# Matmuls of 512 columns issued as two of 256, in two orders, and three orders for the matmuls of an up product

## The chip, the cores and the metric

The kernel runs on one core of one Trainium2 chip. The metric is the time of one execution on the device, in microseconds. Rows of the profile come from one profiled execution; their times count from its first instruction.

## What is computed

One layer of a decoder for 256 tokens of width 2048, all in fp32:

```python
h = rmsnorm(x, g_mix) @ w_in                       # 2048 -> 5728 columns
z, xbc, dt, q, k, v, qi, ki, wi = split(h)
y_ssd = gated_norm(ssd(silu(conv(xbc)), dt), z)    # state space heads
y_att = sparse_attention(q, k, v, qi, ki, wi)      # top 64 keys by an indexer
x = x + concat([y_ssd, y_att]) @ w_out             # 2048 -> 2048
u = rmsnorm(x, g_mlp) @ w_up                       # 2048 -> 8192
return x + square(relu(u)) @ w_down                # 8192 -> 2048
```

Nearly all arithmetic lies in the four products with `w_in`, `w_out`, `w_up` and `w_down`.

## The kernel before

**Exact products in two parts.** TensorE multiplies operands of type fp32r. Each fp32 operand is split into a high part of that type (a cast, on ScalarE) and a low part (the rest, a subtraction on VectorE). For weights `operands` does this, per piece of 128 x 1024 elements that SyncE's DMA queue loads into `raw`: lines 119, 122 and 123 write `raw`, `whi` and `wlo`. There are 4 buffers for `raw` and 5 each for `whi` and `wlo`. A product is then the sum of three terms: high x high, low x high, high x low.

**Two forms of product.** `product` has tokens on partitions: the stationary operand is a slice of 128 tokens of the activations, the moving one is a row of weights, `n` columns wide. For each of 16 steps `kt` over the 2048 terms, and for each half `b` of the tokens, `part` issues three matmuls (lines 141 to 143) into the accumulator `acc[b]`, one PSUM bank of 512 fp32 columns. It serves the input projection (activations `hx`; five blocks of 512 columns, `k`, `q0`, `q1`, `z0`, `z1`, and two of 304, `m0`, `m1`), the output projection (`yah`, `yal` and `ysh`, `ysl`) and the down products (`uh`, `ul`). In the very last block, which has a `tail`, the second half of the tokens is accumulated in two halves of 256 columns in two banks (`acc`, `acc_t`), and the last four steps of each part are done one part after the other, so that each can be added and stored while the next runs.

`product_t` has columns on partitions: the stationary operand is a block of 128 x 128 weights, the moving one the activations, whose high and low parts lie side by side (`x`, 512 columns: 256 high, 256 low). Line 181 multiplies the high weights by all 512 columns, line 182 the low weights by the high 256 columns, into the upper half of the same bank. `total` adds the two halves of the bank later. It serves the blocks `qi` and `xbc` of the input projection (from `hx`) and the up products (from `x2x`, which takes the place of `hx`).

**Order of the work.** TensorE's program is in the order in which the code issues it. Small tasks (norms, transposes, index scores on lines 434 and 435, state space, attention on lines 586 to 611) run beside the large products: `step`, called once per `kt`, moves each of them on. In the MLP no task is left. The MLP goes by quarters `q` of its width: `up(0)`, then `up(q)` and `down(q - 1)` in turn, and `down(3)`. An `up` is eight calls of `product_t` (the first of all is made earlier, as `first`), a `down` four calls of `product`; 32 and 16 in all.

Of the kernel before, what the change touches and what calls it, by code (L numbers as in the profile page):

```python
# [16 lines left out]
P = 128  # L17
D = 2048
T = 256
NB = T // P  # L20
KT = D // P
DFF = 8192
EPS = 1e-6
# [9 lines left out]
# columns of the input projection, in the order of the program's blocks  # L33
# [15 lines left out]
# columns of the per-partition vectors  # L49
# [6 lines left out]
# columns of the vectors that all partitions hold  # L56
# [9 lines left out]
def hymba_kernel(ctx: ExitStack, tc: tile.TileContext, xn, xt, w_in, w_out, w_up, w_down, vcol, vrow, out):  # L66
    nc = tc.nc
# [11 lines left out]
    # ---- what runs beside the large products: each task yields the number of steps to wait, or what has to be done  # L79
    Y = dict(k=20, q=8, cb=11, pv=3, gate0=10, gate1=7, res=3, rr=16, conv=9, sc=2, dec=3, y=3)  # L80
    tasks = []
    done = set()
# [26 lines left out]
    # ---- blocks of a product with 2048 terms; operands in two parts that the tensor engine multiplies exactly  # L109
    def operands(src, n, load=None):  # L110
        """a piece of a block, [128, n], in its two parts"""
# [20 lines left out]
    def product(src, n, left, load=None, tail=None):  # L132
        """tokens on partitions: out[b][:, :n]; with a tail the parts end one after the other: each is handed over as
        (b, columns, out)"""
        acc = accumulators()
        last = KT if tail is None else KT - 4

        def part(kt, out, b, wh, wl):
            s = slice(b * P, (b + 1) * P)
            ah, al = left(kt)  # L140
            nc.tensor.matmul(out, ah[:, s], wh, start=(kt == 0), stop=False)  # L141
            nc.tensor.matmul(out, al[:, s], wh, start=False, stop=False)  # L142
            nc.tensor.matmul(out, ah[:, s], wl, start=False, stop=(kt == KT - 1))  # L143
# [27 lines left out]
    def product_t(src, right):  # L171
        """two blocks of 128 columns on partitions: the two halves' sum is the product"""
        acc = accumulators()
        for i in range(4):
            hi, lo = operands(src[i], 1024)
            c = i % 2
            for k in range(8):
# [3 lines left out]
                nc.tensor.matmul(acc[c], hi[:, s], x, start=(kt == 0), stop=False)  # L181
                nc.tensor.matmul(acc[c][:, T:], lo[:, s], x[:, :T], start=False, stop=(kt == KT - 1))  # L182
# [4 lines left out]
    def total(dst, acc):  # L187
        """dst[:, c, :] = the sum of the two halves"""
# [4 lines left out]
    # ---- the exponential's table, and matrix products until the first operands are there: the engine's clock rises  # L193
# [8 lines left out]
    # ---- loads of the activations, in turn with the first weights  # L202
# [43 lines left out]
    # ---- constants  # L246
# [13 lines left out]
    def rsqrt(dst, src, scale, name, v=nc.vector):  # L260
        """dst = (src * scale + EPS) ** -0.5; the sign of the estimate changes with each step"""
# [13 lines left out]
    # ---- the statistics of the rows  # L275
# [559 lines left out]
```

## Time and profile before

| | |
|---|---|
| median of 3 runs | 1122.08 us (1121.83 to 1122.97) |
| span of the profiled execution | 1121.0 us, first to last instruction |
| TensorE, matmul rows | 1106.8 us, 99% of the span, 5690 matmuls |
| TensorE, weight loads | 935.5 us, 5690 loads |
| VectorE | 705.7 us, 63% |
| ScalarE | 529.8 us, 47% |
| weights loaded | 205.27 MB by DMA, 183 GB/s on average |

The rows come from the profiled execution, whose span is some 1.1 us shorter than the median of the runs. Matmuls overlap, and the end of a matmul's row is modelled; where successive matmuls start is recorded. A line such as L141 is a line of the kernel before. In a row of the timeline, the shape `128*128 128x512` is that of the output's partitions and of the weights, and then of the moving operand: 512 columns.

### The profile page before, as it was taken

What the parts mean: (1) busy time and instruction counts of PE and PEld (TensorE: products, weight loads), DVE (VectorE), ACT (ScalarE), POOL (GpSimd) and SP (SyncE); (2) the same over time, 40 slices, a digit from 0 to 9 for tenths busy, and PEclk for the clock granted to TensorE, in tenths of its full rate; (3) what the DMA queues carried; (4) which work ended last, traced back from release to release, by engine and by line L of the source; (5) the groups of instructions that cost most, each with busy time, mean ns of one, the idle gap of its engine ahead of it and who ended that gap; (6) DMA issues with size and microseconds to landing.
All of it is one profiled execution on the core that took longest, in us unless ns stands there. A gap on an engine that the chain in (4) does not pass through costs nothing.

```text
span 1121.0 us, 14940 instructions
## 1 busy us (share of the span) xinstructions
PE 1106.8 (99%) x5690; PEld 935.5 (83%) x5690; DVE 705.7 (63%) x964; ACT 529.8 (47%) x725; POOL 68.6 (6%) x72
## 2 busy tenths in 40 slices
PE   7999998999999999999999999999999999999998
PEld 5888887788888888888888888888888888888887
DVE  8896889677765566565655446565555565455543
ACT  6555663646665454444443334444334444333331
POOL 7210114122000000000000000000000000000000
PEclk9999999999999999999999999999999999999999
DMA  7665443653465555556566556666666665656662
GB/s 238 210 198 193 156 133 114 225 164 116 147 209 187 187 176 189 188 189 188 189 188 195 189 189 188 188 189 190 195 194 190 188 187 189 189 190 197 212 207 77
DMA packets 61497, 205.27 MB, mean 183 GB/s; under 512 B 7025, under 2 KB 9329, under 8 KB 61425
## 3 DMA queue, kind: packets, MB, share of 16 engines
q1 hardware_dynamic: 61280, 204.26, 57.5%
q8 instruction: 45, 0.74, 0.3%
q14 instruction: 28, 0.22, 0.1%
q10 hardware_dynamic: 144, 0.05, 0.0%
HBM read 202.19 MB, written 2.10 MB: 182 GB/s over the span
## 4 chain that ended last, share of the span: by engine, by line
PE 92%; DVE 4%; DMA 2%; issue 1%; ACT 1%; SPq 0%; POOL 0%; DVEq 0%; ACTq 0%
PE acc L181 26%; PE acc L142 16%; PE acc L143 16%; PE acc L141 16%; PE acc L182 13%; DVE wlo L123 1%; DMA raw<-in_w_in 1%; DVE bc L477 1%; PE ps_y L548 1%; DVE hx L224 1%; DVE sc L441 1%; PE ps_sr L632 0%; PE ps_l L586 0%; PE ps_o L611 0%; PE ps_dec L539 0%
## 5 line engine op out<-in xcount | busy, mean ns | idle before, releaser
L123 DVE TENSOR_TENSOR wlo<-raw,whi 128x1024 fp32r<-128x1024 f32 (+2 forms) x392 | 473.4, 1209 | 381.5 <-ACT whi L122 378.6
L122 ACT CAST whi<-raw 128x1024 fp32r<-128x1024 f32 (+2 forms) x392 | 399.1, 1018 | 516.5 <-PE acc L142 252.6
L181 PE MATMUL acc<-x2x,whi 128*128 128x512 f32 x1024 | 358.8, 393 | 0.0
L182 PE MATMUL acc<-x2x,wlo 128*128 128x256 f32 x1024 | 285.7, 279 | 0.0
L181 PEld LDWEIGHTS acc<-x2x,whi 128*128 128x128 f32 x1024 | 191.9, 187 | 46.0
L142 PE MATMUL acc<-whi,ul 128*128 128x512 f32 (+1 forms) x512 | 199.1, 389 | 0.0
L143 PE MATMUL acc<-wlo,uh 128*128 128x512 f32 (+1 forms) x512 | 199.1, 389 | 0.0
L141 PE MATMUL acc<-whi,uh 128*128 128x512 f32 (+1 forms) x512 | 197.4, 386 | 0.0
L182 PEld LDWEIGHTS acc<-x2x,wlo 128*128 128x128 f32 x1024 | 191.9, 187 | 0.1
L141 PEld LDWEIGHTS acc<-whi,uh 128*128 128x128 f32 x512 | 96.1, 188 | 21.1
L142 PEld LDWEIGHTS acc<-whi,ul 128*128 128x128 f32 x512 | 96.2, 188 | 20.9
L181 PE MATMUL acc<-hx,whi 128*128 128x512 f32 x320 | 113.6, 396 | 0.0
L143 PEld LDWEIGHTS acc<-wlo,uh 128*128 128x128 f32 x512 | 96.2, 188 | 19.1
L142 PE MATMUL acc<-whi,hx 128*128 128x512 f32 (+1 forms) x224 | 84.4, 377 | 5.6 <-DVE hx L224 5.6
L182 PE MATMUL acc<-hx,wlo 128*128 128x256 f32 x320 | 89.4, 279 | 0.0
L143 PE MATMUL acc<-wlo,hx 128*128 128x512 f32 (+1 forms) x224 | 83.3, 372 | 3.1 <-DVE wlo L123 3.1
L141 PE MATMUL acc<-whi,hx 128*128 128x512 f32 (+1 forms) x224 | 85.8, 383 | 0.0
L181 PEld LDWEIGHTS acc<-hx,whi 128*128 128x128 f32 x320 | 60.1, 188 | 13.6
L182 PEld LDWEIGHTS acc<-hx,wlo 128*128 128x128 f32 x320 | 60.0, 188 | 0.0
L142 PEld LDWEIGHTS acc<-whi,hx 128*128 128x128 f32 x224 | 42.2, 188 | 18.8 <-DVE hx L224 12.2
L143 PEld LDWEIGHTS acc<-wlo,hx 128*128 128x128 f32 x224 | 42.2, 188 | 10.7 <-DVE wlo L123 4.2
L141 PEld LDWEIGHTS acc<-whi,hx 128*128 128x128 f32 x224 | 42.2, 188 | 7.7 <-issue 0.7
(224 smaller groups left out, 857.9 us busy)
## 6 DMA issues: line engine op xcount, KB each, us to landing
raw<-in_w_up SPq DMA_DIRECT2D x128, 512.0 KB, 3.6
raw<-in_w_down SPq DMA_DIRECT2D x128, 512.0 KB, 3.6
raw<-in_w_in SPq DMA_DIRECT2D x72, 512.0 KB, 3.5
raw<-in_w_out SPq DMA_DIRECT2D x32, 512.0 KB, 3.5
raw<-in_w_in SPq DMA_DIRECT2D x16, 304.0 KB, 2.9
raw<-in_w_in SPq DMA_DIRECT2D x16, 256.0 KB, 4.0
xT<-in_xt SPq DMA_DIRECT2D x16, 128.0 KB, 3.3
xr<-in_xn SPq DMA_DIRECT2D x4, 512.0 KB, 6.1
```

Source lines behind the costliest of these rows:

```text
L122: nc.scalar.copy(hi[:, s], raw[:, s])
L123: nc.vector.tensor_tensor(lo[:, s], raw[:, s], hi[:, s].bitcast(F32), op=OP.subtract)
L141: nc.tensor.matmul(out, ah[:, s], wh, start=(kt == 0), stop=False)
L142: nc.tensor.matmul(out, al[:, s], wh, start=False, stop=False)
L143: nc.tensor.matmul(out, ah[:, s], wl, start=False, stop=(kt == KT - 1))
L181: nc.tensor.matmul(acc[c], hi[:, s], x, start=(kt == 0), stop=False)
L182: nc.tensor.matmul(acc[c][:, T:], lo[:, s], x[:, :T], start=False, stop=(kt == KT - 1))
L224: nc.vector.scalar_tensor_tensor(hx[:, kt, T:], xT, vcp("g_mix", kt), hx[:, kt, :T].bitcast(F32), op0=OP.mult, op1=OP.subtract)
L441: nc.vector.scalar_tensor_tensor(sc[:, :nk], rl[:, i, :nk], wis[:, b, h:h + 1], neg[:, T - nk:] if first else sc[:, :nk], op0=OP.mult, op1 ...
L477: nc.vector.scalar_tensor_tensor(o[:, j, :], pad[:, j, k:k + T], vcp("conv_w", 12 * k + ct), o[:, j, :], op0=OP.mult, op1=OP.add)
L548: nc.tensor.matmul(pt[:, 64 * i:64 * i + 64], m[i // 4][:, i % 4, :], xdt[:, c, 64 * h:64 * h + 64], start=True, stop=True)
```

## The change

A matmul of 512 columns in `part` is issued as two of 256, each of which names the same stationary operand. Order 0 does the three terms on the first half of the columns and then on the second; order 1 does each term on both halves before the next term. Blocks of 304 columns, and the halves of 256 in the last block, stay single. The input and output projections take order 0; the down products take order 0 in quarters 0 and 2 and order 1 in quarters 1 and 3. In `product_t`, order 0 is the code of before. Order 1 issues the high weights' matmul of 512 columns as two of 256. Order 2 takes two steps `kt` together: two matmuls with high weights, then two with low ones. The up products take order 0 in quarters 0 and 3, order 1 in quarter 1 and order 2 in quarter 2; the blocks `qi` and `xbc` take order 0. Comments and descriptions were removed too.

```diff
-    def product(src, n, left, load=None, tail=None):
+    def product(src, n, left, load=None, tail=None, order=0):
...
             ah, al = left(kt)
-            nc.tensor.matmul(out, ah[:, s], wh, start=(kt == 0), stop=False)
-            nc.tensor.matmul(out, al[:, s], wh, start=False, stop=False)
-            nc.tensor.matmul(out, ah[:, s], wl, start=False, stop=(kt == KT - 1))
+            w = out.shape[1]
+            cs = [slice(0, w // 2), slice(w // 2, w)] if w == 512 else [slice(0, w)]
+            terms = [(ah, wh), (al, wh), (ah, wl)]
+            calls = [(i, c) for c in cs for i in range(3)] if order == 0 else [(i, c) for i in range(3) for c in cs]
+            for at, (i, c) in enumerate(calls):
+                x, y = terms[i]
+                nc.tensor.matmul(out[:, c], x[:, s], y[:, c], start=(kt == 0 and at == 0),
+                                 stop=(kt == KT - 1 and at == len(calls) - 1), skip_group_check=True)
...
-    def product_t(src, right):
+    def product_t(src, right, order=0):
...
-                nc.tensor.matmul(acc[c], hi[:, s], x, start=(kt == 0), stop=False)
-                nc.tensor.matmul(acc[c][:, T:], lo[:, s], x[:, :T], start=False, stop=(kt == KT - 1))
+                end = kt == KT - 1
+                if order == 0:
+                    nc.tensor.matmul(acc[c], hi[:, s], x, start=(kt == 0), stop=False)
+                    nc.tensor.matmul(acc[c][:, T:], lo[:, s], x[:, :T], start=False, stop=end)
+                elif order == 1:
+                    nc.tensor.matmul(acc[c][:, :T], hi[:, s], x[:, :T], start=(kt == 0), stop=False, skip_group_check=True)
+                    nc.tensor.matmul(acc[c][:, T:], hi[:, s], x[:, T:], start=False, stop=False, skip_group_check=True)
+                    nc.tensor.matmul(acc[c][:, T:], lo[:, s], x[:, :T], start=False, stop=end, skip_group_check=True)
+                elif k % 2 == 1:
+                    x0 = right(kt - 1)
+                    s0 = slice((k - 1) * P, k * P)
+                    nc.tensor.matmul(acc[c], hi[:, s0], x0, start=(kt == 1), stop=False)
+                    nc.tensor.matmul(acc[c], hi[:, s], x, start=False, stop=False)
+                    nc.tensor.matmul(acc[c][:, T:], lo[:, s0], x0[:, :T], start=False, stop=False)
+                    nc.tensor.matmul(acc[c][:, T:], lo[:, s], x[:, :T], start=False, stop=end)
...
-            total(r, first if q + j == 0 else product_t(w_up[8 * q + j], x2))
+            total(r, first if q + j == 0 else product_t(w_up[8 * q + j], x2, q % 3))
...
-            acc = product(w_down[4 * q + j], 512, lambda kt: (u[0][:, kt, :], u[1][:, kt, :]), tail=add if end else None)
+            acc = product(w_down[4 * q + j], 512, lambda kt: (u[0][:, kt, :], u[1][:, kt, :]), tail=add if end else None, order=q % 2)
```

## Rows read from the trace of the kernel before

**Rows 1.** Engines of the page: busy us, share of the span, instructions.

```profile
PE 1106.8 (99%) x5690; PEld 935.5 (83%) x5690; DVE 705.7 (63%) x964; ACT 529.8 (47%) x725; POOL 68.6 (6%) x72
```

**Rows 2.** Windows: input projection's last blocks, up products, down products.

```profile
core 0: us, PE busy (x) PEld busy (x) DVE busy (x) ACT busy (x) POOL busy (x), PEclk, DMA share, GB/s
200.00:320.00 120.00, 120.00 (x579) 98.33 (x579) 86.34 (x141) 72.40 (x120) 16.05 (x12) 1.00 0.49 155
410.00:580.00 170.00, 170.00 (x975) 148.23 (x974) 105.94 (x135) 81.18 (x110) 0.00 (x0) 1.00 0.59 187
940.00:1095.00 155.00, 155.00 (x682) 127.29 (x681) 80.12 (x73) 60.21 (x60) 0.00 (x0) 1.00 0.63 199
```

**Rows 3.** Waits: who waited for whom, total us, times, longest us.

```profile
PE acc L142 <- DVE hx L224: 5.6, 15, 1.0
```

**Rows 4.** Timeline of TensorE, a down product: first and last of 54 matmuls.

```profile
599.64 0.39 PE L143 MATMUL acc<-wlo,uh 128*128 128x512 f32 x1
...
611.77 0.39 PE L142 MATMUL acc<-whi,ul 128*128 128x512 f32 x1
```

**Rows 5.** Timeline of TensorE, the last down product: rounds of nine, then halves alone.

```profile
1105.25 0.39 PE L141 MATMUL acc<-whi,uh 128*128 128x512 f32 x1
...
1109.35 0.39 PE L141 MATMUL acc<-whi,uh 128*128 128x512 f32 x1
...
1114.83 0.28 PE L141 MATMUL acc<-whi,uh 128*128 128x256 f32 x1
...
1116.08 0.28 PE L143 MATMUL acc<-wlo,uh 128*128 128x256 f32 x1
...
1117.44 0.28 PE L143 MATMUL acc_t<-wlo,uh 128*128 128x256 f32 x1
```

**Rows 6.** Timeline of TensorE, input projection: 30 of 304 columns, 27 of 512.

```profile
45.91 0.30 PE L143 MATMUL acc<-wlo,hx 128*128 128x304 f32 x1
...
50.00 0.30 PE L142 MATMUL acc<-whi,hx 128*128 128x304 f32 x1
...
206.68 0.39 PE L143 MATMUL acc<-wlo,hx 128*128 128x512 f32 x1
...
212.77 0.40 PE L142 MATMUL acc<-whi,hx 128*128 128x512 f32 x1
```

**Rows 7.** Timeline of TensorE, output projection: first and last of 28 matmuls.

```profile
329.81 0.39 PE L141 MATMUL acc<-whi,ysh 128*128 128x512 f32 x1
...
335.99 0.39 PE L141 MATMUL acc<-whi,ysh 128*128 128x512 f32 x1
```

**Rows 8.** Timeline of TensorE, an up product: the first matmuls and the 37th.

```profile
519.61 0.39 PE L181 MATMUL acc<-x2x,whi 128*128 128x512 f32 x1
519.84 0.28 PE L182 MATMUL acc<-x2x,wlo 128*128 128x256 f32 x1
519.96 0.39 PE L181 MATMUL acc<-x2x,whi 128*128 128x512 f32 x1
...
525.91 0.39 PE L181 MATMUL acc<-x2x,whi 128*128 128x512 f32 x1
```

**Rows 9.** Timeline of TensorE, index scores: first and fifth of five matmuls.

```profile
114.20 0.28 PE L434 MATMUL ps_s<-kih,qis 128*128 128x256 f32 x1
...
114.68 0.28 PE L434 MATMUL ps_s<-kih,qis 128*128 128x256 f32 x1
```

**Rows 10.** Groups by form, one line of three: count, busy us, mean ns, idle.

```profile
L141 PE MATMUL acc<-whi,uh 128*128 128x512 f32 x496 | 193.0, 389 | 0.0
...
L141 PE MATMUL acc<-whi,hx 128*128 128x512 f32 x160 | 66.2, 414 | 0.0
...
L141 PE MATMUL acc<-whi,yah 128*128 128x512 f32 x64 | 25.9, 405 | 0.0
```

**Rows 11.** The instructions of line 435: weight loads and their duration in ns.

```profile
L435 PEld LDWEIGHTS ps_s<-kil,qis x32: 187/189/192, 108.8 to 169.8; 128*128 128x128 f32 x32
```

**Rows 12.** Pieces of the chain, start us, us: plain fp32 matmuls of 256 and 128 columns.

```profile
272.87 1.73 PE ps_o L611 x8
...
298.07 0.87 PE ps_pt L603 x8
```

## The prediction

> **What bounds the kernel now.** I read the table of engines first. TensorE's matmul rows cover 99% of the span [rows 1]. A busy matmul row is a model of overlapping instructions, so the number to read is not its length but the distance from one start to the next. Before that, the stretches: in the input projection's last four blocks, in the up products and in the down products TensorE has no gap at all, its granted clock is 1.00 (the 2.4 GHz level), and VectorE and ScalarE are busy for 39 to 72% of the time [rows 2]. So a nanosecond more or less per matmul goes straight into the end time, in nearly all of the kernel. The one place among the changed products where it does not is the first block ("k"): there TensorE waits 15 times for the low part of the activations, `hx` from VectorE [rows 3], so its 96 matmuls have cover.
>
> Then the starts, in the timeline. Durations in this text are first start to last start over the number of steps between, all in the profiled execution (span 1121.0 us; the three timed runs have a median of 1122.08, so about 1.1 us lies around the span, and I carry that over).
>
> - Down products, 512 columns: 599.64 to 611.77 is 53 steps, 228.9 ns each [rows 4].
> - The end of the kernel already runs 256-column matmuls in a down product, because the last block hands its parts over one by one. 1114.83 to 1117.44 is 23 steps: 113.5 ns. Further ahead, where three matmuls of 512 alternate with six of 256, a round takes (1109.35 - 1105.25)/3 = 1.367 us; less 3 x 228.9 that leaves 113.3 ns for one of 256 [rows 5]. I take 113.4.
> - Input projection, 512 columns: 206.68 to 212.77 is 26 steps, 234.2 ns. The 304-column blocks of the same product: 45.91 to 50.00 is 29 steps, 141.0 ns [rows 6].
> - Output projection: 329.81 to 335.99 is 27 steps, 228.9 ns [rows 7].
> - Up products: a 512 and a 256 together, 519.61 to 525.91, 18 pairs, 350.0 ns [rows 8].
> - The index scores, 256 columns, each weight used twice in a row and the halves of a bank in turn: 114.20 to 114.68 is four steps, 120 ns [rows 9].
>
> So two halves are not simply one whole: in the down products 2 x 113.4 = 226.8 is below 228.9, and the index rate doubled, 240, is far above it. The whole question is which of these rows the new 256-column matmuls resemble.
>
> **Part 1: the split in `part`.** What is split are all matmuls of width 512; 304 and the tail's 256 stay. Counts come from the groups by form, three lines each: down 3 x 496 = 1488, output projection 3 x (64 + 64) = 384 (the group for `ysh` is as large as that for `yah`), input projection 3 x 160 = 480 [rows 10]. Every half loads its weights anew: the score matmuls on line 435 use the weights that line 434 has just used, and have 32 loads of their own for 32 matmuls [rows 11]. So loads double with the matmuls. The tail's rows contain that already: one load for each 256, and at the seam between two halves the same `uh` twice.
>
> *Down, order 0 (quarters 0 and 2, 768) and order 1 (quarters 1 and 3, 720).* Order 0 is what the tail does, three terms on one half and then three on the other, same operands; only the bank is shared now. I take 113.4: 226.8 - 228.9 = -2.1 ns. Order 1 sends each weight twice, in turn to the two halves, which in this kernel only the index scores do, at 120 with other operands. Bounds for it: -2.1 and +11.1 ns. The operands are the tail's and the loads are the same, so it is nearest to the tail: -2.1. Together 1488 x -2.1 = -3.1 us (order 1 at its upper end: +8.0 instead of -1.5 us).
>
> *Output projection.* No 256 there, but its 512 has the down products' pace to 0.1 ns: 384 x -2.1 = -0.8 us; bounds -0.8 and 384 x 11.1 = +4.3.
>
> *Input projection.* Its pace is slower, so the tail's price need not hold. A line through its own 304 (141.0) and 512 (234.2) has 0.448 ns per column and gives 119.5 at 256; the up products' 256, between its neighbours, shows 0.12 us at the rows' two decimals [rows 8]. I take 119: 238 - 234.2 = +3.8 ns. The block "k" (96) has cover: a half less is done before the wait for `hx`, and VectorE sets the pace. If that cover were gone it would add 96 x 3.8 = 0.4 us. The other four blocks, 384: +1.5 us. Bounds: 113.4 gives -2.8, 120 gives +2.2.
>
> **Part 2: the up products.** Quarters 0 and 3 (order 0) are unchanged. Order 1 in quarter 1: 8 products of 32 groups, 256 groups, each 512 + 256 becoming three of 256. Cost of one: the slope between the down products' two widths is (228.9 - 113.4)/256 = 0.451 ns per column; 768 columns of a pair make 346.4, the remaining 3.6 ns are shared by two matmuls, so 256 columns cost 115.5 + 1.8 = 117.3, and three cost 351.9 against 350.0. 256 x 1.9 = +0.5 us. Bounds: three at 113.4 give -2.5, three at 120 give +2.6. Order 2 in quarter 2 only regroups four matmuls, two of 512 and then two of 256; count, columns and loads stay, and `hi` and `lo` are used later, not earlier. I take 0; were each switch of width what costs the 3.6 ns, half of the switches would go: 256 x -1.8 = -0.5 us, and I allow the same upwards.
>
> Nothing else moves. The weights' DMAs, the casts and subtractions and the tasks' places are per piece or per row of `kt`, and those did not change. VectorE and ScalarE get the same work in the same time; a half-matmul frees nothing earlier, as a piece of weights is still free after its last matmul.
>
> **Sum:** -3.1 - 0.8 + 1.5 + 0.5 + 0 = -1.9 us on 1121.0, a span of 1119.1; with what lies around it, about 1120.2. I forecast 1120.
>
> A rule that speaks against even this small gain: the Trainium skill, in "TensorE: Matmul & The Clock Gate", section "Back-to-back issue gap", gives a stream of warm matmuls as columns over 2.4 plus 2.5 ns, so that each split would cost 2.5 ns and the change some 6 us. Here the two halves are 2.1 ns below the whole, and a 512 is at 228.9 where the rule has 215.8; the trace disagrees on both.
>
> **The rivals.**
>
> 1. *The halves run at the tail's pace everywhere.* For: the tail shows the same 113.4 between matmuls of 512 and among halves alone. Against: the 256s of the up products and of the index scores are slower. Input -2.8, up order 1 -2.5, order 2 -0.5, down and output -3.9: -9.7 us, 1112.4. Chance 0.12.
> 2. *Order 1 pays the index rate:* a weight sent twice, or the two halves of a bank in turn, costs 120. For: rows 9. Against: there the step from a repeated weight to a new one is as long as the step between repeats. Down order 1 then +8.0 instead of -1.5: 1129.7, slower. From 114.7 ns for a 256 there the forecast's gain is gone (1440 x 1.3 = 1.9 us), from 116.3 the kernel is slower by over 0.2%. Chance 0.10.
> 3. *A fixed price for each instruction.* Plain fp32 pieces of the chain show a little of one: eight of 256 columns take 1.73 us, 216.3 ns each, eight of 128 take 0.87, 108.8 each [rows 12]: two halves cost 1.3 ns more than a whole. The 304 and 512 of the input projection, drawn down to no columns, leave 141.0 - 304 x 0.448 = 4.8 ns. Were 4.8 the price of every added matmul: (1488 + 384 + 384 + 256) x 4.8 = +12.1 us, 1134. Against: rows 5. Chance 0.05. Set against a cost of nothing per added matmul it decides from 0.9 ns (2512 x 0.9 = 2.2 us).
> 4. *The tail is special* because its halves lie in two banks, and every new 256 costs 119.5: down and output 1872 x 10.1 = +18.9, input +1.8, up +2.2: 1145. Against: 1114.83 to 1116.08, 11 steps that all write one bank, are 113.6 ns apart. Chance 0.05.
>
> **How the numbers follow.** My own case has 0.68. Its terms of the input and up products move it by 3 us either way, so its own range is 1117 to 1123. What a measurement of this kernel can tell from no change is about 0.2%, 2.2 us: faster means below 1119.8. My case lies just beside that line: I give 0.31 of its 0.68 to faster, 0.33 to the same, 0.04 to slower. With the rivals: faster 0.31 + 0.12 = 0.43, same 0.33, slower 0.04 + 0.20 = 0.24. The range for 8 in 10 takes my case, most of rival 1, and the lower prices of rivals 2 and 3 (order 1 partly at the index rate): 1113 to 1127.
>
> **What would show it.** In the timeline after, steps between starts: down, quarters 0 and 2: 113.4; quarters 1 and 3: 113.4 if I am right, about 120 under rival 2; output projection 113.4; input projection near 119; up quarter 1 near 117.3, a group of three at 352; up quarter 2 700 for four, as before. TensorE should stay without gaps in all of these stretches and its loads count as many as its matmuls; a gap at regular distances would be a thing I have not priced. The prediction is wrong if the down products' halves are not below 114.4, where their gain is gone, or if the input projection's halves keep to the tail's pace.

## The result, and the profile after

The changed kernel takes 1135.47 us (median of 4 runs, 1134.7 to 1136.5) against 1122.02 us for the kernel before in the same comparison (1121.83 to 1122.97): a ratio of 1.012, with a 95% interval of 1.0107 to 1.0133. It is slower, and lies outside the range of 1113 to 1127. The profiled executions have spans of 1132.9 and 1121.0 us. A single run lies some 1.8 us above its own span, and the profiled execution before was one of the slower ones, so the medians differ by 13.5 us and the two spans by 11.9. What follows accounts for the 11.9; the first row of its table is where the two differences part.

The table of engines of the kernel after, beside [rows 1]:

```profile
PE 1121.2 (99%) x8298; PEld 1063.8 (94%) x8298; DVE 705.2 (62%) x964; ACT 529.8 (47%) x725; POOL 68.7 (6%) x72
```

TensorE has 2608 instructions more, which is the count of the prediction (1488 + 384 + 480 + 256), and as many weight loads. The other engines do the same work in the same time. The windows of the kernel after follow: the three stretches of [rows 2], then 60 us inside each of the four down quarters.

```profile
core 0: us, PE busy (x) PEld busy (x) DVE busy (x) ACT busy (x) POOL busy (x), PEclk, DMA share, GB/s
200.00:320.00 120.00, 120.00 (x958) 116.08 (x957) 85.09 (x139) 71.93 (x119) 16.40 (x12) 1.00 0.49 154
410.00:580.00 170.00, 170.00 (x1189) 158.67 (x1188) 104.73 (x137) 79.85 (x110) 0.00 (x0) 1.00 0.60 185
940.00:1095.00 155.00, 155.00 (x1294) 153.93 (x1293) 79.20 (x74) 59.36 (x59) 0.00 (x0) 1.00 0.62 194
600.00:660.00 60.00, 60.00 (x512) 60.00 (x511) 29.94 (x28) 22.61 (x22) 0.00 (x0) 1.00 0.61 187
780.00:840.00 60.00, 60.00 (x532) 60.00 (x531) 31.10 (x28) 23.38 (x23) 0.00 (x0) 1.00 0.61 193
960.00:1020.00 60.00, 60.00 (x511) 60.00 (x511) 29.91 (x27) 22.69 (x22) 0.00 (x0) 1.00 0.59 185
1050.00:1110.00 60.00, 60.00 (x512) 60.00 (x511) 30.09 (x27) 22.43 (x22) 0.00 (x0) 1.00 0.67 206
```

In all of these windows TensorE is without a gap and its granted clock is 1.00, as before. The last four rows hold the surprise: the same number of columns per matmul, on the same kind of operands, gives 532 matmuls in 60 us in quarter 1 and 511 or 512 in the others. Quarter 1 is order 1, but so is quarter 3.

The timeline of TensorE gives the steps and where each stretch begins. First the start of the first down product in the kernel before, and of the up product behind it:

```profile
586.81 0.40 PE L141 MATMUL acc<-whi,uh 128*128 128x512 f32 x1
...
674.72 0.40 PE L181 MATMUL acc<-x2x,whi 128*128 128x512 f32 x1
```

Then the kernel after. Rows with x2 are two matmuls of one form that the view shows as one.

```profile
193.89 0.40 PE L147 MATMUL acc<-whi,hx 128*128 128x256 f32 x2
...
208.28 0.40 PE L147 MATMUL acc<-whi,hx 128*128 128x256 f32 x2
...
211.80 0.40 PE L147 MATMUL acc<-whi,hx 128*128 128x256 f32 x2
...
314.19 0.47 PE L147 MATMUL acc<-whi,yah 128*128 128x256 f32 x1
...
329.76 0.28 PE L147 MATMUL acc<-whi,ysh 128*128 128x256 f32 x1
...
334.00 0.28 PE L147 MATMUL acc<-whi,ysh 128*128 128x256 f32 x1
...
408.31 0.40 PE L188 MATMUL acc<-x2x,whi 128*128 128x512 f32 x1
...
539.84 0.28 PE L191 MATMUL acc<-x2x,whi 128*128 128x256 f32 x1
...
542.72 0.28 PE L191 MATMUL acc<-x2x,whi 128*128 128x256 f32 x1
...
590.96 0.28 PE L147 MATMUL acc<-whi,uh 128*128 128x256 f32 x1
...
599.79 0.28 PE L147 MATMUL acc<-whi,uh 128*128 128x256 f32 x1
...
602.97 0.28 PE L147 MATMUL acc<-whi,uh 128*128 128x256 f32 x1
...
681.41 0.40 PE L197 MATMUL acc<-x2x,whi 128*128 128x512 f32 x1
...
720.28 0.39 PE L197 MATMUL acc<-x2x,whi 128*128 128x512 f32 x1
...
722.40 0.39 PE L197 MATMUL acc<-x2x,whi 128*128 128x512 f32 x1
...
771.87 0.39 PE L147 MATMUL acc<-whi,uh 128*128 128x256 f32 x2
...
799.75 0.39 PE L147 MATMUL acc<-whi,uh 128*128 128x256 f32 x2
...
802.92 0.28 PE L147 MATMUL acc<-wlo,uh 128*128 128x256 f32 x1
...
858.91 0.40 PE L188 MATMUL acc<-x2x,whi 128*128 128x512 f32 x1
...
948.52 0.28 PE L147 MATMUL acc<-whi,uh 128*128 128x256 f32 x1
...
1126.60 0.28 PE L147 MATMUL acc<-whi,uh 128*128 128x256 f32 x1
...
1129.19 0.28 PE L147 MATMUL acc_t<-whi,ul 128*128 128x256 f32 x1
```

Steps, worked out as in the prediction (last start less first start, over the steps between):

- Down, quarter 0: 599.79 to 602.97 is 27 steps, 117.8 ns. Quarters 2 and 3 have the same.
- Down, quarter 1: 799.75 to 802.92 is 28 steps, 113.2 ns.
- The tail of the last block, whose matmuls were not touched: 1126.60 to 1129.19 is 22 steps, 117.7 ns. Before it was 113.5 [rows 5].
- Output projection: 329.76 to 334.00, 36 steps, 117.8 ns.
- Input projection: 208.28 to 211.80, 30 steps, 117.3 ns.
- Up product, order 1: 539.84 to 542.72 is eight groups of three halves, 360.0 ns each, where a pair took 350.0 [rows 8].
- Up product, order 2: 720.28 to 722.40 is three groups of four, 706.7 ns each. By the starts in the trace, to the nanosecond, the four steps take 232.5, 231.7, 117.5 and 125.0 ns on the average; in order 0 a 512 takes 232.0 and a 256 takes 118.0. So the extra 6.7 ns lie behind the second low matmul, ahead of the next 512.

I call 113.3 the short step and 117.8 the long step from here on. From the starts of the stretches, before against after:

| Stretch | before, us | after, us | difference | predicted |
|---|---|---|---|---|
| all ahead of the last four input blocks | 195.37 | 193.89 | -1.48 | 0 |
| last four input blocks | 119.60 | 120.30 | +0.70 | +1.5 |
| output projection | 91.75 | 94.12 | +2.37 | -0.8 |
| up quarters 0 and 1 (1: order 1) | 180.09 | 182.65 | +2.56 | +0.5 |
| down quarter 0 | 87.91 | 90.45 | +2.54 | -0.8 |
| up quarter 2 (order 2) | 89.61 | 90.45 | +0.85 | 0 |
| down quarter 1 | 87.90 | 87.04 | -0.86 | -0.8 |
| up quarter 3 | 89.64 | 89.61 | -0.03 | 0 |
| down quarters 2 and 3, to the end | 179.16 | 184.37 | +5.21 | -1.5 |

The sum is +11.9. The first row is scatter, not the change. In it, block `k` takes 31.7 us from its first matmul to the first of the next block, where it took 32.4 before; but after_again, a second execution of the changed kernel (below), has 32.6, and the kernels below that leave `k` whole have 31.8 to 32.5. No effect of the split shows there. TensorE waits for `hx` as before, in the view of the waits, beside [rows 3]:

```profile
PE acc L147 <- DVE hx L242: 5.1, 14, 1.2
```

The rest of the first row is in blocks that the change leaves alone; it took 158.2 us before and 157.2 after, and lies between 157.1 and 158.5 in the profiled executions of all kernels here. Without the first row the table adds up to +13.3 us, close to the 13.5 by which the medians differ.

### The profile page after: what moved, and what is told of

Same layout as the page of the kernel before. It is cut to its first block, busy times and chain, and to the rows that moved or that the text cites. A ratio compares the mean times of both kernels' runs of the same rounds, so it can differ in the third digit from the quotient of the medians.

```text
span 1132.9 us, 20157 instructions
## 1 busy us (share of the span) xinstructions
PE 1121.2 (99%) x8298; PEld 1063.8 (94%) x8298; DVE 705.2 (62%) x964; ACT 529.8 (47%) x725; POOL 68.7 (6%) x72
## 4 chain that ended last, share of the span: by engine, by line
PE 94%; DVE 3%; DMA 1%; issue 1%; ACT 1%; SPq 0%; POOL 0%; DVEq 0%; ACTq 0%
PE acc L147 49%; PE acc L188 16%; PE acc L189 8%; PE acc L192 3%; PE acc L191 3%; PE acc L193 3%; PE acc L198 3%; PE acc L197 3%; PE acc L200 1%; PE acc L199 1%; DMA raw<-in_w_in 1%; DVE wlo L123 1%; DVE bc L495 1%; PE ps_y L566 1%; DVE sc L459 1%
## 5 line engine op out<-in xcount | busy, mean ns | idle before, releaser
L147 PE MATMUL acc<-whi,ul 128*128 128x256 f32 x1008 | 242.0, 279 | 0.0
L147 PE MATMUL acc<-whi,uh 128*128 128x256 f32 x1008 | 241.9, 278 | 0.0
L147 PE MATMUL acc<-wlo,uh 128*128 128x256 f32 x1008 | 241.5, 278 | 0.0
L188 PE MATMUL acc<-x2x,whi 128*128 128x512 f32 x512 | 179.6, 393 | 0.0
L147 PEld LDWEIGHTS acc<-whi,uh 128*128 128x128 f32 x1008 | 172.1, 188 | 0.0
L147 PE MATMUL acc<-whi,hx 128*128 128x256 f32 (+1 forms) x768 | 149.3, 292 | 5.1 <-DVE hx L242 5.1
L188 PEld LDWEIGHTS acc<-x2x,whi 128*128 128x128 f32 x512 | 95.9, 187 | 22.8
L147 PE MATMUL acc<-wlo,hx 128*128 128x256 f32 (+1 forms) x384 | 110.3, 287 | 1.8 <-DVE wlo L123 1.8
L189 PEld LDWEIGHTS acc<-x2x,wlo 128*128 128x128 f32 x512 | 95.9, 187 | 0.0
L192 PE MATMUL acc<-x2x,whi 128*128 128x256 f32 x256 | 72.4, 283 | 0.0
L191 PE MATMUL acc<-x2x,whi 128*128 128x256 f32 x256 | 71.8, 280 | 0.0
```

The source lines that it names most:

```text
L147: nc.tensor.matmul(out[:, c], x[:, s], y[:, c], start=(kt == 0 and at == 0), stop=(kt == KT - 1 and at == len(calls) - 1), skip_group_chec ...
L191: nc.tensor.matmul(acc[c][:, :T], hi[:, s], x[:, :T], start=(kt == 0), stop=False, skip_group_check=True)
L192: nc.tensor.matmul(acc[c][:, T:], hi[:, s], x[:, T:], start=False, stop=False, skip_group_check=True)
```

## The experiments

The down products are more than half of the loss, and the puzzle: one code, two steps. Four theories stood in the expectations. **Entry theory:** what TensorE did just before a stream of halves sets its step, and the stream keeps it. **Order theory:** order 0 or order 1 sets it. **Chance theory:** it falls anew in each execution. **Place theory:** it goes with the buffer that holds `uh` and `ul`, which change places with every quarter. The quarters follow each other as up 0, up 1, down 0, up 2, down 1, up 3, down 2, down 3.

Kernels run in rounds have a ratio with its 95% interval; the others were run once beside their profile, and of these I use the stretches and steps. With whole matmuls down 0 takes 87.9 us; all halves at the short step make that 87.0, at the long step 90.5. The runs come from several chips; lead_a, lead_b and lead_c share one, lead_d and lead_e another, and the steps of down_o0's quarters were the same on two chips (lead512 and slots on the second).

**after_again.** The changed kernel a second time, unchanged.

> The changed kernel once more, for a second trace. Entry theory (the step of a stream of 256-column matmuls is settled by what TensorE did just before the stream and is then kept): every stretch repeats its step, quarter 1's down product 113.3 ns, the three others 117.8. Chance theory (each execution falls into one of the two steps anew): at least one of the four down products is at the other step; its time moves by 3.3 us (768 matmuls of 256 columns x 4.4 ns) for each.

1135.6 us, span 1133.8. Every stretch from the output projection on has its length of the first profile within 0.06 us. The chance theory falls: which quarter is short belongs to the program. The repeated runs further below agree: the four of down_o0 lie within 0.7 us and the nine of lead_d within 1.3, and one quarter at the other step would move a run by 3.4. The other runs with leads were executed once each.

**down_o1 and down_o0.** Only the down products are split, in order 1 throughout or in order 0 throughout. The diff is down_o1; down_o0 has `order=0` in the last line.

```diff
-    def product(src, n, left, load=None, tail=None, order=0):
+    def product(src, n, left, load=None, tail=None, order=None):
...
-            cs = [slice(0, w // 2), slice(w // 2, w)] if w == 512 else [slice(0, w)]
+            cs = [slice(0, w // 2), slice(w // 2, w)] if w == 512 and order is not None else [slice(0, w)]
...
-            total(r, first if q + j == 0 else product_t(w_up[8 * q + j], x2, q % 3))
+            total(r, first if q + j == 0 else product_t(w_up[8 * q + j], x2))
...
-            acc = product(w_down[4 * q + j], 512, lambda kt: (u[0][:, kt, :], u[1][:, kt, :]), tail=add if end else None, order=q % 2)
+            acc = product(w_down[4 * q + j], 512, lambda kt: (u[0][:, kt, :], u[1][:, kt, :]), tail=add if end else None, order=1)
```

> Only the down products are split, all in order 1; projections and up products are those of before. Order theory (order 1 runs at 113.3 ns, order 0 at 117.8): 1488 x (226.6 - 228.9) = -3.4 us, 1118.6, all four quarters at 113.3. Entry theory: each down product is entered from an up product as before, which in the changed kernel led to 117.8 in quarter 2, so 117.8 in all: 1488 x 6.7 = +10.0 us, 1132.

> Only the down products are split, all in order 0. Order theory: 117.8 ns in all quarters, 1488 x 6.7 = +10 us, 1132, and 13 us slower than all in order 1. Entry theory: also 117.8, also 1132, no different from all in order 1. The rule of the prediction (113.4 as in the tail): 1118.6.

down_o1: 1128.89 us (ratio 1.0058, 1.0043 to 1.0073). down_o0: 1128.85 us (1.0058, 1.0041 to 1.0075). In both, down 0 is 2.54 us longer, down 1 is 0.86 shorter and down 2 and 3 are 5.22 longer. The windows of down_o1 in quarters 0 and 1:

```profile
600.00:660.00 60.00, 60.00 (x512) 60.00 (x511) 30.11 (x27) 22.85 (x22) 0.00 (x0) 1.00 0.56 186
780.00:840.00 60.00, 60.00 (x532) 60.00 (x531) 31.12 (x28) 23.45 (x23) 0.00 (x0) 1.00 0.58 194
```

Order 1 has both steps, and order 0 has the same two in the same places: the order theory falls. Quarter 1 is the short one although the up product ahead of it is now the same as ahead of the others, so the simplest form of the entry theory, that the kind of up product decides, falls as well. The 1132 us expected from it was 3 us too long, by that quarter.

**swap.** The changed kernel with the orders of the down products exchanged, `order=(q + 1) % 2`.

> The changed kernel with the two orders exchanged between the quarters of the down products: 0 where 1 was and 1 where 0 was. Order theory: quarters 0 and 2 (now order 1) at 113.3 ns, quarters 1 and 3 at 117.8. Entry theory: nothing moves, quarter 1 stays at 113.3 behind the up product in order 2, the others at 117.8, time within 1 us of the changed kernel.

1135.49 us, span 1133.7. All stretches are those of the changed kernel; quarter 1 is short in order 0 too.

**lead512.** down_o0 with the first step `kt` of each quarter's first block left whole, so that six matmuls of 512 lead in.

```diff
-            cs = [slice(0, w // 2), slice(w // 2, w)] if w == 512 and order is not None else [slice(0, w)]
+            cs = [slice(0, w // 2), slice(w // 2, w)] if w == 512 and order is not None and kt >= whole else [slice(0, w)]
...
-            acc = product(w_down[4 * q + j], 512, lambda kt: (u[0][:, kt, :], u[1][:, kt, :]), tail=add if end else None, order=0)
+            acc = product(w_down[4 * q + j], 512, lambda kt: (u[0][:, kt, :], u[1][:, kt, :]), tail=add if end else None, order=0, whole=1 if j == 0 else 0)
```

> Only the down products split, all in order 0, but for the first of the 64 steps over the terms in each quarter: its six matmuls stay 512 wide. Entry theory (the step is settled where the stream of halves begins): behind matmuls of 512 the halves lock at 113.3 ns, as they did in the last block of the kernel before, in all four quarters: 1464 x (226.6 - 228.9) = -3.4 us, span 1117.6, run 1118.8. Place theory (it hangs on where uh and ul lie): no difference from the run without the lead, quarters 0, 2 and 3 at 117.8, quarter 1 at 113.3, 1128.9.

1128.48 us (1.0055, 1.0039 to 1.0072): a miss. The steps are those of down_o0. A few whole matmuls in front do not clear whatever sets the step.

**half_b1.** down_o0 with only the second token block split, so that halves run between whole matmuls everywhere: the condition for the split becomes `w == 512 and order is not None and b == 1`.

> Only the down products split, and there only the second half of the tokens: in every step three matmuls of 512 and then six of 256, which is what the last block of the kernel before did for most of its length. Entry theory: each run of halves is entered from 512s, so 1.367 us for each step as there, against 6 x 228.9 = 1.373: 244 steps x -6.4 ns = -1.6 us, 1120.5. If halves are at 117.8 whatever stands before them: 244 x 6 x 3.35 ns = +4.9 us, 1127.

1125.18 us (1.0029, 1.0018 to 1.004): a miss again. The halves take 117.8 ns in quarters 0, 2 and 3 and 113.3 in quarter 1, six in a row between whole ones; the stretches differ by +1.28, -0.43 and +2.68 us, half of down_o0's. So the step is not lost when the stream is broken by 512s. The tail of the kernel before is just such a mixture [rows 5]: that it ran at 113.3 is one of two possible outcomes, not its nature.

**slots.** down_o0 with the two buffers of `uh` and `ul` exchanged, by one more allocation ahead of the first quarter.

```diff
+        if q == 0:
+            for nm in ("uh", "ul"):
+                z = mlp.tile([P, KT, T], F32R, name=nm)
+                nc.gpsimd.memset(z[:, 0, :].bitcast(F32), 0.0)
```

> Only the down products split, all in order 0, with the two buffers of uh and ul exchanged between the quarters (a buffer is cleared in part and given back ahead of quarter 0, so that quarters 0 and 2 use the second and 1 and 3 the first). Place theory: the step goes with the buffer, quarters 0 and 2 at 113.3 ns, quarter 1 at 117.8; span about 1125.3. Entry theory: quarter 1 stays the fast one, span as without the exchange, 1127 to 1128.

1129.59 us, span 1127.8; quarter 1 is still the short one. The place theory falls.

**lead_small.** down_o0 with one plain fp32 matmul of 128 columns, whose result is unused, ahead of each down quarter. It is two instructions.

```diff
     def down(q, u):
+        pt = mp("ps_lead")
+        nc.tensor.matmul(pt[:, :P], ident, ident, start=True, stop=True)
```

> Only the down products split, all in order 0, with one small plain fp32 product of 128 columns into a spare bank ahead of each down product (its result isn't used). Entry theory: the shift at the entry changes the step of at least one quarter; which one isn't foreseen; each quarter that changes moves the span by 3.4 us. Place theory: no quarter changes, and the span grows by under 1 us for the eight small matmuls.

1129.59 us, span 1127.8. Quarter 1 has turned long and quarter 3 short. The timeline of lead_small where quarters 1 and 3 begin:

```profile
766.06 0.38 PE L784 MATMUL ps_lead<-ident 128*128 128x128 f32 x2
...
766.41 0.28 PE L147 MATMUL acc<-whi,ul 128*128 128x256 f32 x1
...
767.47 0.28 PE L147 MATMUL acc<-whi,ul 128*128 128x256 f32 x1
...
1037.06 0.38 PE L784 MATMUL ps_lead<-ident 128*128 128x128 f32 x2
...
1037.40 0.28 PE L147 MATMUL acc<-whi,ul 128*128 128x256 f32 x1
...
1038.19 0.28 PE L147 MATMUL acc<-wlo,uh 128*128 128x256 f32 x1
```

766.41 to 767.47 is nine steps, 117.8 ns; 1037.40 to 1038.19 is seven, 112.9 ns. The step is there within the first matmuls and then holds for the 90 us of the quarter. With nothing else changed, 0.14 us of other work at each entry turned two of the four quarters over. In this form, that what runs ahead decides, the entry theory holds; which of the leads turned quarter 1 this run doesn't tell.

**lead_a, lead_b.** Other plain fp32 leads, to find which one gives which step.

```diff
     def down(q, u):
+        n = (256, 0, 192, 128)[q]
+        if n:
+            pt = mp("ps_lead")
+            nc.tensor.matmul(pt[:, :n], ident, neg[:, :n], start=True, stop=True)
```

That is lead_a. In lead_b the leads are `for n in ((64,), (), (128, 128), (128,))[q]`, each with the same matmul.

> Only the down products split, all in order 0, with one plain fp32 product into a spare bank ahead of quarters 0, 2 and 3, of 256, 192 and 128 columns (results unused; quarter 1 has none). Entry theory: quarter 1 at 113.3 ns as without leads, quarter 3 at 113.3 as in the run with a small lead everywhere; quarters 0 and 2 at one of the two steps, 113.3 or 117.8, nothing between. Span 1120.6 if both are slow, 3.4 us less for each fast one. If a lead only costs its own time: 1128.

> As the run before, with other leads: 64 columns ahead of quarter 0, twice 128 ahead of quarter 2, 128 ahead of quarter 3. Entry theory: quarters 1 and 3 at 113.3 ns, quarters 0 and 2 at either step; span 1124.2 at most, 3.4 us less for each of the two that is fast.

lead_a: 1130.94 us, span 1129.2; quarter 1 is short, the others long, quarter 3 against the expectation (whose 1120.6 us for both slow is a slip: its own terms give about 1124). lead_b: 1133.59 us, span 1131.8; all four are long, quarter 1 too, which has no lead in either kernel. Up to that point the two programs differ only in the width of quarter 0's lead, 256 or 64 columns, some 180 us earlier. The windows of quarter 1, lead_a first, then lead_b:

```profile
780.00:840.00 60.00, 60.00 (x532) 60.00 (x532) 31.12 (x29) 23.23 (x22) 0.00 (x0) 1.00 0.61 195
780.00:840.00 60.00, 60.00 (x512) 60.00 (x511) 30.34 (x28) 22.04 (x21) 0.00 (x0) 1.00 0.57 186
```

So, by these two executions, what sets the step is carried through a whole down quarter and the up product behind it. In both kernels and in lead_small, a lead of 128 columns stands ahead of quarter 3 behind a long quarter 2; with `ident` as its moving operand it left quarter 3 short (lead_small), with `neg` long (lead_a, lead_b). The width of a lead alone does not tell which step follows.

**lead_c, lead_d, lead_e.** Leads in the operands' own type, fp32r, of 256 columns, one instruction each. The counts ahead of quarters 0 to 3 are (1, 0, 2, 1) in lead_c, (1, 1, 1, 0) in lead_d and (1, 2, 1, 0) in lead_e.

```diff
     def down(q, u):
+        for _ in range((1, 0, 2, 1)[q]):
+            pt = mp("ps_lead")
+            nc.tensor.matmul(pt[:, :T], gtr, box[0][:, 0, :T], start=True, stop=True)
```

> As the runs before, with leads of the stream's own form, 256 columns in fp32r: one ahead of quarters 0 and 3, two ahead of quarter 2. Entry theory: a lead of the same form only lengthens the stream, so the step that it had before is kept: quarters 0 and 2 at 117.8 ns, quarter 3 too, quarter 1 at 113.3, span 1127 to 1128. If any matmul ahead shifts the entry: quarter 3 or another changes by 3.4 us.

> Only the down products split, all in order 0, with one lead of 256 columns in fp32r ahead of quarters 0, 1 and 2. Entry theory: quarter 0 at 113.3 ns as in the run with one such lead. Behind a fast quarter 0, quarter 1 is entered the way quarter 0 was (the same steps of the up product ahead), so one lead makes it 113.3 too, and so on to quarter 2; quarter 3 follows on without a seam and keeps it. All fast: 1121.0 - 3.4 + 0.4 for the leads = 1118.0 of span, about 1119.2, faster than before by 0.25%. If the step can't be had by a lead of one kind in every quarter: 3.4 us more for each slow one, 1122.6 or above.

> As the run before, but with two leads ahead of quarter 1. Entry theory with the observation that an odd number of such leads was fast in quarter 0 and an even one was not: quarter 1 at 117.8 ns, quarter 0 at 113.3. A lead that merely fills the time: no difference between the two runs but its own 0.118 us.

lead_c: 1129.35 us, span 1127.6; quarter 0 has turned short, which I had not expected, and quarters 1 to 3 are long. lead_e, with two leads ahead of quarter 1: 1129.52 us, span 1127.7; quarter 0 short, 1 to 3 long. lead_d, with one lead ahead of each of the first three: 1119.14 us (9 runs, 1118.78 to 1120.08) against 1121.86 for the kernel before (13 runs), ratio 0.9975 (0.9965 to 0.9985). All four quarters are short. The windows of lead_d:

```profile
600.00:660.00 60.00, 60.00 (x532) 60.00 (x531) 30.92 (x28) 23.44 (x23) 0.00 (x0) 1.00 0.59 194
780.00:840.00 60.00, 60.00 (x532) 60.00 (x531) 30.92 (x28) 23.39 (x23) 0.00 (x0) 1.00 0.62 195
960.00:1020.00 60.00, 60.00 (x532) 60.00 (x531) 31.08 (x29) 23.23 (x22) 0.00 (x0) 1.00 0.60 193
1050.00:1110.00 60.00, 60.00 (x532) 60.00 (x531) 26.87 (x24) 20.07 (x19) 0.00 (x0) 1.00 0.52 173
```

The lead of quarter 0 and the first halves behind it, in the timeline of lead_d:

```profile
586.07 0.28 PE L785 MATMUL ps_lead<-x2x,gtr 128*128 128x256 f32 x1
586.19 0.28 PE L147 MATMUL acc<-whi,uh 128*128 128x256 f32 x1
586.30 0.28 PE L147 MATMUL acc<-whi,ul 128*128 128x256 f32 x1
...
589.93 0.28 PE L147 MATMUL acc<-whi,uh 128*128 128x256 f32 x1
```

586.30 to 589.93 is 32 steps, 113.4 ns. The down stretches come out at -0.87, -0.85 and -1.59 us, and the three leads add 0.12, 0.12 and 0.08 to the up stretches that they end. Three matmuls whose results are unused take a split that costs 6.6 us (down_o0) to one that gains 2.7 in the median: the sign of this change in the down products hangs on what runs at the entries. lead_d beats both kernels.

**up_o1.** The kernel before with the up products of quarters 1, 2 and 3 in order 1, everything else whole.

```diff
-            total(r, first if q + j == 0 else product_t(w_up[8 * q + j], x2, q % 3))
+            total(r, first if q + j == 0 else product_t(w_up[8 * q + j], x2, 1 if q else 0))
```

> The kernel before with only the up products of quarters 1, 2 and 3 in order 1; nothing is split in the projections and down products. A fixed price of order 1: +2.56 us in each of the three, as in the changed kernel's quarter 1 (three halves in 360 ns), span 1121.0 + 7.7 = 1128.7. Entry theory carried over to this stream: one of the three quarters has another step than 120 ns, down to 3 x 113.3 = 340 against 350 for the pair, which would be -2.6 us there.

1129.98 us, span 1128.2. The three up stretches are 2.56, 2.56 and 2.50 us longer: 256 groups of 360.0 instead of 350.0 ns each time, whatever ran ahead of them. This cost came out the same at all three entries. The run holds one thing more that was not expected: its down products are whole, and yet the untouched tail of the last block has turned long:

```profile
1121.89 0.28 PE L147 MATMUL acc<-whi,uh 128*128 128x256 f32 x1
...
1124.60 0.28 PE L147 MATMUL acc_t<-wlo,uh 128*128 128x256 f32 x1
```

That is 23 steps, 117.8 ns, where the kernel before has 113.5 in the same code [rows 5]. The stretch of down quarters 2 and 3 is 0.60 us longer.

**out_o0, out_lead1, out_lead2.** Only the output projection is split, in order 0, with no, one or two fp32r matmuls of 256 columns ahead of it. The diff is out_lead1; out_lead2 has `range(2)` and out_o0 only the last line. The input projection, the up and the down products are whole.

```diff
+            if j == 0:
+                for _ in range(1):
+                    pt = mp("ps_lead")
+                    nc.tensor.matmul(pt[:, :T], gtr, yah[:, 0, :T], start=True, stop=True)
-            spawn(residual(j, product(w_out[j], 512, y_left)), f"res{j}")
+            spawn(residual(j, product(w_out[j], 512, y_left, order=0)), f"res{j}")
```

> Only the output projection is split (order 0); input projection, up and down products are as before. Both theories expect the long step here, as nothing ahead of the output projection differs from the kernel with all splits except the input projection's halves: 117.8 ns per half, stretch 91.75 + 2.4 = 94.1 us, kernel about 1124.4. If the unsplit input projection ahead hands on another state, the entry theory allows the short step, 113.3 ns: stretch 90.9 us, kernel about 1121.2; the operand theory (this product's operands always take the long step) doesn't.

> As the kernel with only the output projection split, and one fp32r matmul of 256 columns ahead of it, whose result is unused. Entry theory: one lead turns the step over, so that if it is long without a lead it is 113.3 ns here, the stretch 384 x 4.5 = 1.7 us shorter than without the lead less 0.1 for the lead. Operand theory: 117.8 ns, 94.2 us as without it.

> As the kernel with only the output projection split, and two fp32r matmuls of 256 columns ahead of it. Entry theory: turned over twice, so the same step as without a lead. Operand theory: 117.8 ns in any case.

Spans 1122.9, 1123.4 and 1122.2 (single runs of 1124.8, 1125.23 and 1123.96 us). From the first matmul of the product to the first up product it is 94.11, 93.89 and 93.89 us; the 0.2 us are a step of 0.30 that falls behind the first matmul in the one and behind the lead in the others. The timeline of out_lead1 at the entry:

```profile
314.87 0.47 PE L749 MATMUL ps_lead<-yah,gtr 128*128 128x256 f32 x1
315.17 0.28 PE L147 MATMUL acc<-whi,yah 128*128 128x256 f32 x1
...
316.94 0.28 PE L147 MATMUL acc<-whi,yah 128*128 128x256 f32 x1
```

15 steps of 118.0 ns, as without the lead. The leads left the step long, so the form in which one lead turns it over is not shown here. But the operand theory, that this product's operands always take the long step, falls: transposes of other tasks break the product into nine stretches, five of 96 to 180 matmuls and four of 12, and one or two of the four run at the short step, on the same operands. In out_o0:

```profile
367.89 0.28 PE L147 MATMUL acc<-whi,yal 128*128 128x256 f32 x1
...
369.02 0.28 PE L147 MATMUL acc<-wlo,yah 128*128 128x256 f32 x1
```

That is ten steps, 113.0 ns. The five larger stretches have the long step in all three kernels and in the changed one; what decides it there stays open.

## Why the prediction was wrong

- **What held.** TensorE sets the end without a gap, at an unchanged clock; the added instructions and loads are counted rightly; nothing on another engine or queue moved; in block `k` no cost of the split shows, as its cover had it. So the whole result is in the steps, and the steps are what I priced wrongly.
- **The step that failed** is the one that took 113.4 for a half of the down products because the tail of the same product has it, with the same form, operands and loads [rows 5]. In the changed kernel that very tail runs at 117.7. The same code in the last block of up_o1 has 117.8 with whole matmuls ahead of it. The price was not a property of the form but one of two values, and the 256s of the trace of before held only the one. The prediction's own sign of being wrong, halves that are not below 114.4, came in quarters 0, 2 and 3. The term of -3.1 us became +6.9: 1104 old matmuls in quarters 0, 2 and 3 at 2 x 117.8 - 228.9 = +6.7 ns each (+7.4), 384 in quarter 1 at -2.3 (-0.9), and 96 halves of the old tail at +4.4 (+0.4). lead_d, in which the halves do have the price of the prediction, gives -3.3 in the same stretches: the sum was right for that value. With all terms as measured the prediction's sum reads +6.9 + 2.4 + 0.7 + 2.6 + 0.85 = some +13.4 us in place of -1.9.
- **Output projection:** the same value was carried over because the 512s of both products take 228.9; it measured 117.8 and +2.4 us instead of -0.8, inside the bounds given. The runs don't show why it is long here; it isn't the operands (out_o0).
- **Input projection:** the right sign, too dear: 117.3 in the stretch shown, and +0.7 instead of +1.5. Two halves at 117.3 against 234.2 would give only +0.2 over 384 matmuls; where the other 0.5 arises, in a stretch with the tasks' matmuls in between, the runs don't show.
- **Up products, order 1:** +2.6 instead of +0.5, at the upper bound of three at 120. The mean price of 117.3 drawn from the slope between two widths didn't hold; up_o1 shows 360.0 per group at three entries.
- **Up products, order 2:** +0.85, outside of the bounds of 0.5 either way: 128 groups times 6.7 ns. I had taken a regrouping of the same matmuls as free. In this quarter it isn't, and by the sign fewer changes of width cost rather than save. Order 2 was not run by itself.
- **The rivals.** The tail's pace everywhere fell with quarter 0. The index rate for order 1 is refuted where it was put, in the down products (down_o1 equals down_o0 to 0.01 us), though its price, 120 for each of three, is what order 1 of the up products pays. A fixed price per instruction can't be both +6.7 and -2.3 ns per split. The tail as a special case came nearest in its number (119.5 against 117.8), but its reason fell: quarter 1 has both halves in one bank at 113.3, and the tail with its two banks now has 117.7. The bounds that I gave order 1, -2.1 and +11.1 ns, hold both outcomes to 0.2 ns; order 0 had no upper bound at all, because the tail was so near a neighbour.

The Trainium skill's rule in "TensorE: Matmul & The Clock Gate", section "Back-to-back issue gap", which the prediction set aside, would have had the sign right: 2.5 ns for each split. The prediction took it for that of a stream; the section calls it the gap of an isolated matmul, and has about 131 ns for a matmul of 512 columns in a sustained stream of loads and matmuls. The runs show +6.7 or -2.3 ns for each split of the down products instead, depending on what ran ahead, and no stretch has 131 ns for a 512.

**What stays open:** what in the chip the step is locked to. Shown in the down products are that the step is there from the first matmuls of a quarter and holds to its end, through whole matmuls (half_b1, lead512); that one lead in fp32r turns quarter 0 from long to short (lead_c and lead_d against down_o0); and, by one execution of each, that a lead ahead of quarter 0 decides over quarter 1 through other products (lead_a against lead_b). The leads were tried without a rule, and lead512, lead_a and lead_c each did something else than expected in at least one quarter.

The traces do hold a sign that was not used. By the starts, to the nanosecond, the 512s of an up product in order 0 take 230 or 231 ns and 232 to 235 ns in turn. Wherever no lead stands between, a down quarter is long behind an up product whose last 512 took the shorter of the two, and short behind the longer: so in all 25 cases where 256s followed to show it, the tail behind whole matmuls included. With one fp32r lead it is the reverse, in all six; behind an up product with plain fp32 leads, or with two in fp32r, the quarter was long in all nine. The kernel before has the shorter ahead of quarter 0 and the longer ahead of quarters 1 and 2, so its trace held the two entries though not the two prices. This was read off afterwards: it is a sign and not yet a cause, no run tested it, and it says nothing of the output projection.

## What to carry to other kernels

In a kernel that TensorE bounds without a gap, a matmul's step read off one stretch of the trace is a sample, not a price: when a change is worth 2 ns a matmul, both values (here 113.3 and 117.8) belong into the sum, each with its own outcome. After any edit to the matmul stream, look at the steps of stretches that were not edited too; if one of them moved, try a single unused matmul of the stream's own type at its entry before giving the edit up; here it turned quarter 0 of the down products but not the output projection. Equal column counts did not make splitting or regrouping free: here it cost 6.7 ns per split, 10.0 per group of three and 6.7 per group of four, and paid 2.3 per split only in quarters at the short step.

## What the runs showed of the hardware that was not expected

- One stream of fp32r matmuls of 256 columns, each with its own weight load, at a granted clock of 1.00, runs at 113.3 or at 117.8 ns per matmul. The value was the same in both profiled executions of the changed kernel, quarter by quarter, and differs between programs that differ in one matmul ahead of the stream (quarter 0 of down_o0 and lead_d).
- Two orders of the same halves, weights in turn or halves in turn, cost the same to 0.01 us per quarter of 768 matmuls in the down products.
- Whole matmuls of 512 settle at 228.9 ns on the average in both cases (half_b1), so they hide the difference but for the first few: in lead512 the first six of quarter 0 take 236, 228, 237, 231, 232 and 226 ns ahead of long halves, those of quarter 1 231, 229, 232, 225, 230 and 231 ahead of short ones.
- Two of 512 and then two of 256 take 706.7 ns, in turn 700.0: in up quarter 2, grouping by width cost time.
